# A trunk of two layers on one core: another home for projected blocks, and a PSUM bank for turned tiles

## The chip, the core and the metric

The kernel runs on one core of one Trainium2 chip. The metric is the device time of one execution in microseconds; less is better. TensorE (PE) does matrix products and transposes, VectorE (DVE), ScalarE (ACT) and GpSimd (POOL) the rest, and each engine takes its own instructions in order. DMA queues move data; the queue named SP is issued by SyncE, another here by GpSimd.

## What is computed

256 tokens of width 2048 pass through two layers, each a mixer, cross-attention into 256 memory tokens and a gated feed-forward network, all with a residual and an RMSNorm ahead. The first layer's mixer is split: eight heads of a gated linear recurrence (HGRN2) and eight of a gated delta rule (GDN). The second's is Mamba-2 (SSD, 8 groups). Weights are fp32. Cut to the mixers:

```python
def hgrn2_gdn_mixer(u, w_in, ...):
    a_q, a_f, a_i, a_g, b_q, b_k, b_v, b_g, b_beta, b_a = _split(matmul(u, w_in), HY_SIZES)
    log_f = log(lb + (1.0 - lb) * sigmoid(a_f));  k_a = (1.0 - lb) * sigmoid(-a_f)
    o_a = gated_head_norm(hgrn2_chunked(silu(a_q), k_a, a_i, log_f), hgrn_norm, a_g)
    qkv = silu(causal_depthwise_conv(concatenate([b_q, b_k, b_v]), gdn_conv_w))
    ...
    o_b = gated_head_norm(gated_delta_chunked(l2norm(q_b), l2norm(k_b), v_b, beta, g), gdn_norm, b_g)
    return matmul(concatenate([o_a, o_b]), w_out)
def gated_delta_chunked(...):
    t_mat = triangular_solve(eye + a_mat, eye)
...
def mamba2_mixer(u, w_in, ...):
    z, xbc, dt_raw = _split(matmul(u, w_in), ...)
    xbc = silu(causal_depthwise_conv(xbc, conv_w) + conv_b)
    ...
    return matmul(rmsnorm(y * silu(z), norm_w), w_out)
```

## The kernel before

**Weights.** `wtiles` (L158) streams every weight as raw tiles `wr` of 128x1024 fp32, four buffers, on the SP queue. `split` (L155) makes two of each: ScalarE casts to the short format `wh`, VectorE takes the rest, `wl`. Activations `u` are split likewise. `xstat` multiplies a block of 512 columns in 96 matmuls (16 k tiles, two token halves, three products xh·wh, xl·wh, xh·wl) into two PSUM tiles `acc`. These accumulation matmuls (helper `mm`, L121) are nearly all of TensorE's work. Helpers hide callers: L121 is every matmul, L124 every two-operand product (`tt`), L127 every product of three (`stt`).

**Pools.** PSUM has four banks for `acc` (pool pa) and four in rotation for everything else (pool pm, function `psb`, name `mx` in the rows). In SBUF the small work buffers `b2` (shown as `b`) rotate over four; `tmp` and `sm` over two; `raw`, `vt`, `kq`, `cv`, `gate`, `X`, `XT`, `D` have one each.

**Projected blocks.** `rows` (L355) lets ScalarE scale the two accumulators into two `b2` tiles. `turned` (L272) transposes one such block in two halves on TensorE, eight transposes in all, each half into one of pm's banks. `columns` (L369) makes both halves and returns them. A convolution (`conv`, L347: one ScalarE copy and three VectorE products per 128 channels), or sigmoids, or copies then read them.

**A delta-rule chain.** Each call of `gdn(g)` handles four heads. Products of kq give M (tile MD) and its decays; a scratch write (L554) and a reload (L556) on GpSimd's queue bring the 16x16 diagonal blocks together as U; thirty small VectorE products (15 steps) invert them; a copy (L567), a write (L571) and loads (L573) give X and XT. Then three levels of matmuls join blocks: XT·B, a copy R by ScalarE (L585), X·R and R·X, and a subtraction on VectorE. The products with v, and in `finish` with the decays (`w,MD`, `w,D`), follow, then `head_norm` (L421, L429) and the transposes of its result (`cst,b`). The first chain is `gdn(0)`, the second `gdn(1)`; then the recurrence `hgrn(0)` and `hgrn(1)`, whose six levels take differences of cv into `tmp` on VectorE, an exponential on ScalarE (L660) and two products with kq on GpSimd.

**What sets the order.** The program is written in order of the formulas. A planner with a timeline of its own then decides, engine by engine, in which order instructions stand, and lets the buffers of a pool rotate by it. It mixes accumulation matmuls of later blocks into a chain where it judges a wait.

Of the kernel before, what the change touches and what calls it, by code (L numbers as in the profile page):

```python
# [9 lines left out]
F32 = mybir.dt.float32  # L10
# [3 lines left out]
AF = mybir.ActivationFunctionType  # L14
ALU = mybir.AluOpType
AX = mybir.AxisListType
PSUM = bass.MemoryType.PSUM

P = 128
D = 2048  # L20
T = 256
# [57 lines left out]
def trunk(ctx: ExitStack, tc: tile.TileContext, A: dict, out: bass.AP):  # L79
    nc = tc.nc  # L80
    pe, act, dve, pool = nc.tensor, nc.scalar, nc.vector, nc.gpsimd
# [4 lines left out]
    mp = ctx.enter_context(tc.tile_pool(name="m", bufs=1))  # L86
    dp = ctx.enter_context(tc.tile_pool(name="d", bufs=1, space=bass.MemoryType.DRAM))
    pa = ctx.enter_context(tc.tile_pool(name="pa", bufs=4, space=PSUM))
    pm = ctx.enter_context(tc.tile_pool(name="pm", bufs=4, space=PSUM))


    cols = cp.tile([P, NCOLS], F32, name="cols")
# [23 lines left out]
    def col(name, i=0, n=1):  # L116
        o = COLS[name][0] + i
        return cols[:, o:o + n]
# [10 lines left out]
    def t4(tag, shape, dt=F32):  # L129
        return mp.tile(shape, dt, name=tag, tag=tag, bufs=BUFS.get(tag, 1))  # L130

    def psb(shape=None):
        return pm.tile(shape or [P, 512], F32, name="mx", tag="mx")
# [135 lines left out]

    h = [cp.tile([P, 2, 512], F32, name=f"h{nb}") for nb in range(4)]  # L270

    def turned(src, i):  # L272

        ps = psb([P, 2, T])
        for x in range(2):
            c = 2 * i + x
            for a in range(2):
                pe.transpose(ps[:, x, a * P:(a + 1) * P], src[a][:, c * P:(c + 1) * P], ident)  # L278
        return ps
# [69 lines left out]
    def conv(c, x, w):  # L349

        act.activation(c, x, AF.Copy, scale=w[:, 3:4])  # L351
        for s in range(1, 4):
            stt(c[:, s:T], x[:, 0:T - s], w[:, 3 - s:4 - s], c[:, s:T], ALU.mult, ALU.add)

    def rows(N, W, n0, func=AF.Copy, first=None):  # L355

        accs = xstat(W, n0, 512, N.u)
        if first:
            first()
        r = N.column()  # L360
        o = [t4("b2", [P, 512]) for _ in range(2)]
        for a in range(2):
            act.activation(o[a], accs[a], func, scale=r[:, a:a + 1])  # L363
            if func == AF.Sigmoid:
                stt(o[a], accs[a], r[:, a:a + 1], o[a], ALU.mult, ALU.mult)
        return o

    def columns(N, W, n0, func=AF.Copy):

        o = rows(N, W, n0, func)  # L370
        return [turned(o, i) for i in range(2)]

    def heads_by_token(N, W, n0, c0):

# [77 lines left out]
    def hybrid(N, nxt):  # L452
        W = ("hy_w_in", 0)
# [17 lines left out]
            return decay_parts(gT, 8), bt  # L471

        def conv_in(j, g, o):
            o_rows = rows(N, W, 4096 + 1024 * j + 512 * g, first=constants_in if (j, g) == (1, 0) else None)
            ps = [turned(o_rows, i) for i in range(2)]
            for m in range(4):
                conv(o[:, m, :], ps[m // 2][:, m % 2], col("gdn_conv", 4 * (8 * j + 4 * g + m), 4))

# [141 lines left out]
        def hgrn(g):  # L622
            kq = t4("kq", [P, 2, 4, T])
            lf = t4("tmp", [P, 4, T])
            fs = t4("raw", [P, 4, T])
            for i, ps in enumerate(columns(N, W, 1024 + 512 * g)):
                act.activation(lf[:, 2 * i:2 * i + 2], ps, AF.Sigmoid)
                act.activation(fs[:, 2 * i:2 * i + 2], ps, AF.Sigmoid, scale=-1.0)
            for m in range(4):
                dve.tensor_scalar(kq[:, 0, m], fs[:, m], lb[:, 1, 4 * g + m:4 * g + m + 1], None, op0=ALU.mult)  # L630
            for i, ps in enumerate(columns(N, W, 512 * g, AF.Sigmoid)):
                act.copy(kq[:, 1, 2 * i:2 * i + 2], ps)
            gate = gate_rows(N, W, 3072 + 512 * g, AF.Sigmoid)
            G = t4("cv", [P, 4, T])
# [80 lines left out]

    def xattn(layer, N, nxt):
        q = t4("cv", [P, 4, T])
        for i, ps in enumerate(columns(N, ("xa_wq", layer), 0)):
            act.copy(q[:, 2 * i:2 * i + 2], ps)
        def load_mem(nb):  # L720
            raw = wp.tile([P, 4, T], F32, name="wr", tag="wr", bufs=4)
# [2 lines left out]

        M = Norm(("norm_mem", 16 * layer), load_mem, mem_r[0] if mem_r else None)
        k = t4("X", [P, 4, T])
        for i, ps in enumerate(columns(M, ("xa_wk", layer), 0)):
            act.copy(k[:, 2 * i:2 * i + 2], ps)
        if not mem_r:
            mem_r.append(cp.tile([P, 2], F32, name="mem_r"))  # L730
# [69 lines left out]
    def ssd(N, nxt):  # L800
# [18 lines left out]

        def bc(half):  # L820

            t = [t4(tag, [P, 4, T]) for tag in ("vt", "raw")]
            for j in range(2):
                ps = columns(N, W, 8192 + 1024 * j + 512 * half)
                for x in range(4):
                    b = 32 + 8 * j + 4 * half + x
                    conv(t[j][:, x], ps[x // 2][:, x % 2], col("ssd_conv", 4 * b, 4))
                    act.activation(t[j][:, x], t[j][:, x], AF.Silu, bias=col("ssd_conv_b", b))
            return t

        def group(g, bct):
# [7 lines left out]
            act.copy(cb[:, 1], p0[:, 1])  # L839
            tt(dve, cb[:, 2], p1, le, ALU.mult)  # L840
            xc = t4("cv", [P, 4, T])
            px = columns(N, W, 4096 + 512 * g)
            for m in range(4):
                conv(xc[:, m], px[m // 2][:, m % 2], col("ssd_conv", 4 * (4 * g + m), 4))
                act.activation(xc[:, m], xc[:, m], AF.Silu, bias=col("ssd_conv_b", 4 * g + m))
            xd = t4("w", [P, 2, 8, 64])
            for a in range(2):
                ps = psb([P, 8, 64])
# [5 lines left out]
            for half in range(2):  # L854
# [8 lines left out]
                for x in range(2):  # L863
                    m = 2 * half + x
                    stt(y[:, m], xc[:, m], col("ssd_d", 4 * g + m), ps[:, x], ALU.mult, ALU.add)
            for i, z in enumerate(columns(N, W, 512 * g, AF.Silu)):
                tt(dve, y[:, 2 * i:2 * i + 2], y[:, 2 * i:2 * i + 2], z, ALU.mult)
            hi, lo = utiles()
            for m in range(4):
# [144 lines left out]
```

## Time and profile before

| | us |
|---|---|
| median of three runs | 2999.55 (2998.99 to 3001.03) |
| the profiled execution | 2998.11 |
| its span in the trace | 2996.3 |
| TensorE busy | 2944.5 |
| first delta-rule chain, 160.92 to 201.26 | 40.34 |
| second, 297.51 to 344.46 | 46.95 |
| SSD stage, 730 to 2215 | 1485.00 |

The trace holds one execution. A row gives its start and duration, the operation with the tiles it writes and reads (out<-in), a count, and in square brackets the idle time of the engine ahead of it and what ended that. A stretch that is as long as its PE busy time has no TensorE idle. The granted clock stands as a share of full speed.

### The profile page before, as it was taken

Reading aid. Unit: us, or ns where it says so; the run is one execution under the profiler, and the core shown is the slowest. Engines: PE = TensorE matmul, PEld = TensorE weight load, DVE = VectorE, ACT = ScalarE, POOL = GpSimd, SP = SyncE. Lnnn points to the kernel's source line nnn. Section 1 sums busy time; section 2 is a strip of 40 time slices with the busy share of each in tenths; the row PEclk is TensorE's granted clock in tenths of the full one; section 3 lists DMA queues with packets and bytes.
Section 4 is the critical chain, followed back from the end, with each engine's and each line's share of the span. In section 5 each row is a group of like instructions: output and inputs, shape, how many; then the busy total and the mean of one; then the engine's idle time right before and its main releaser. Section 6 shows DMA issues by size and latency. Waiting matters only on the chain.

```text
span 2996.3 us, 36590 instructions
## 1 busy us (share of the span) xinstructions
PE 2944.5 (98%) x13948; PEld 2450.2 (82%) x13948; DVE 1735.7 (58%) x2154; ACT 1486.4 (50%) x1916; POOL 262.7 (9%) x209
## 2 busy tenths in 40 slices
PE   9989899999999999999999999999999999999998
PEld 7877788887888888888888888888888888888887
DVE  6647566666455455545667655667665554545455
ACT  7435455465443444344556645666555444443444
POOL 1011223020000000000012300232000000000000
PEclk9999899999999999999999999999999999999999
DMA  7535245564655666665555555545666666666664
GB/s 277 177 116 178 69 136 163 177 209 140 191 190 190 193 188 188 195 190 188 175 176 157 156 186 187 163 153 164 185 201 188 190 189 191 192 188 192 193 189 148
DMA packets 152160, 533.35 MB, mean 178 GB/s; under 512 B 16592, under 2 KB 22864, under 8 KB 151984
## 3 DMA queue, kind: packets, MB, share of 16 engines
q1 hardware_dynamic: 150096, 526.15, 56.3%
q0 software_dynamic: 1472, 4.59, 0.5%
q8 instruction: 109, 1.79, 0.2%
q14 instruction: 67, 0.55, 0.1%
q10 hardware_dynamic: 416, 0.27, 0.0%
HBM read 526.49 MB, written 4.46 MB: 177 GB/s over the span
## 4 chain that ended last, share of the span: by engine, by line
PE 94%; DMA 2%; DVE 1%; ACT 1%; issue 1%; POOL 0%; DVEq 0%; SPq 0%; ACTq 0%; POOLq 0%
PE acc L121 86%; PE mx L121 6%; PE mx L278 2%; DMA XT<-scratch 0%; DVE wl L124 0%; DMA scratch<-b 0%; POOL tmp L124 0%; DMA wr<-in_memT 0%; DMA b<-scratch 0%; ACT b L585 0%; PE mx L850 0%; DMA scratch<-MD 0%; DVE b L124 0%; PE mx L429 0%; DMA wr<-in_hy_w_in 0%
## 5 line engine op out<-in xcount | busy, mean ns | idle before, releaser
L121 PE MATMUL acc<-wh,u 128*128 128x512 f32 (+1 forms) x7904 | 2450.4, 390 | 7.0 <-ACT wh L156 7.0
L124 DVE TENSOR_TENSOR wl<-wr,wh 128x1024 fp32r<-128x1024 f32 x980 | 1243.2, 1272 | 1055.1 <-ACT wh L156 1052.8
L121 PEld LDWEIGHTS acc<-wh,u 128*128 128x128 f32 x7904 | 1480.1, 188 | 305.2 <-ACT wh L156 7.8
L156 ACT CAST wh<-wr 128x1024 fp32r<-128x1024 f32 x980 | 1029.1, 1052 | 1165.1 <-PE acc L121 1104.3
L121 PE MATMUL acc<-wl,u 128*128 128x512 f32 (+1 forms) x3952 | 1536.5, 389 | 1.3 <-DVE wl L124 1.3
L121 PEld LDWEIGHTS acc<-wl,u 128*128 128x128 f32 x3952 | 744.4, 188 | 150.8 <-DVE wl L124 2.9
L124 POOL TENSOR_TENSOR tmp<-gh,cst 128x512 fp32r<-128x512 f32 x36 | 39.9, 1110 | 1317.9 <-ACT gh L156 884.7
L124 POOL TENSOR_TENSOR tmp<-tmp,kq 128x512 f32<-128x512 f32 x32 | 56.9, 1805 | 136.5 <-ACT tmp L660 124.4
L127 DVE SCALAR_TENSOR_TENSOR cv<-mx,cols,cv 128x255 f32<-128x255 f32 (+2 forms) x120 | 52.5, 475 | 13.6 <-ACT cv L351 13.0
L124 DVE TENSOR_TENSOR h<-h,acc 128x512 f32<-128x512 f32 (+1 forms) x84 | 52.2, 655 | 9.6 <-PE acc L121 9.4
L363 ACT ACTIVATE b<-acc,r 128x512 f32<-128x512 f32 x66 | 43.9, 687 | 27.0 <-PE acc L121 16.9
L124 POOL TENSOR_TENSOR tmp<-gl,cst 128x512 fp32r<-128x512 f32 x36 | 52.4, 1457 | 0.1
L127 DVE SCALAR_TENSOR_TENSOR u<-mx,cols,u 128x256 fp32r<-128x256 f32 x96 | 42.7, 478 | 14.4 <-ACT u L436 7.3
L299 ACT ACTIVATE u<-mx,cols 128x256 fp32r<-128x256 f32 x80 | 34.2, 469 | 20.9 <-PE mx L278 17.9
L278 PE MATMUL mx<-cst,b 128*128 128x128 f32 x272 | 39.1, 274 | 0.0
L124 DVE TENSOR_TENSOR u<-mx,u 128x512 fp32r<-128x512 f32 x48 | 31.0, 683 | 13.9 <-ACT u L156 13.9
L124 DVE TENSOR_TENSOR X<-X,mx 128x512 f32<-128x512 f32 x28 | 18.5, 683 | 32.9 <-PE mx L121 32.9
L278 PEld LDWEIGHTS mx<-cst,b 128*128 128x128 f32 x272 | 32.3, 141 | 5.9 <-issue 1.4
L156 ACT CAST u<-mx 128x512 fp32r<-128x512 f32 x48 | 26.0, 591 | 22.3 <-PE mx L121 11.7
L124 POOL TENSOR_TENSOR MD<-MD,b 128x1536 f32<-128x1536 f32 x8 | 35.0, 4371 | 7.8 <-ACT MD L403 7.8
L121 PE MATMUL mx<-tmp,mr 128*128 128x512 f32 x108 | 32.7, 406 | 0.0
L121 PEld LDWEIGHTS mx<-tmp 128*128 128x128 f32 x240 | 28.8, 196 | 2.5 <-POOL tmp L124 1.9
(259 smaller groups left out, 1281.1 us busy)
## 6 DMA issues: line engine op xcount, KB each, us to landing
wr<-in_ffn_w_gate SPq DMA_DIRECT2D x176, 512.0 KB, 3.7
wr<-in_ffn_w_up SPq DMA_DIRECT2D x176, 512.0 KB, 3.6
wr<-in_ffn_w_down SPq DMA_DIRECT2D x176, 512.0 KB, 3.7
wr<-in_ssd_w_in SPq DMA_DIRECT2D x162, 512.0 KB, 3.8
wr<-in_hy_w_in SPq DMA_DIRECT2D x130, 512.0 KB, 4.2
wr<-in_ssd_w_out SPq DMA_DIRECT2D x64, 512.0 KB, 3.9
wr<-in_hy_w_out SPq DMA_DIRECT2D x32, 512.0 KB, 3.7
wr<-in_xa_wq SPq DMA_DIRECT2D x16, 512.0 KB, 3.7
```

Source lines behind the costliest of these rows:

```text
L121: pe.matmul(o, lhsT=lhsT, rhs=rhs, start=start, stop=stop, skip_group_check=True)
L124: e.tensor_tensor(o, a, b, op=op)
L127: dve.scalar_tensor_tensor(o, a, s, b, op0=op0, op1=op1)
L156: act.copy(hi, src)
L278: pe.transpose(ps[:, x, a * P:(a + 1) * P], src[a][:, c * P:(c + 1) * P], ident)
L299: act.activation(hi[:, c], ps[:, x], AF.Copy, scale=g)
L363: act.activation(o[a], accs[a], func, scale=r[:, a:a + 1])
```

## The change

The change gives the projected blocks and the turned tiles other buffers:

- `rows` writes its block into one tile `raw` ([128, 2, 512], a single buffer) in place of two `b2` tiles.
- PSUM's pool pm goes from four banks to three, and a new pool pt has one, for the turned tiles (name `tn`).
- `columns` becomes a generator: it turns the first half, hands it to its reader, then turns the second into the same bank. All its readers loop over it.
- In `hgrn` the tile that was `raw` goes: the sigmoid is written into kq and scaled there. In SSD's `bc` the second tile moves from `raw` to `gate`.

```diff
--- before.py
+++ after.py
@@ -86,7 +86,8 @@
     mp = ctx.enter_context(tc.tile_pool(name="m", bufs=1))
     dp = ctx.enter_context(tc.tile_pool(name="d", bufs=1, space=bass.MemoryType.DRAM))
     pa = ctx.enter_context(tc.tile_pool(name="pa", bufs=4, space=PSUM))
-    pm = ctx.enter_context(tc.tile_pool(name="pm", bufs=4, space=PSUM))
+    pt = ctx.enter_context(tc.tile_pool(name="pt", bufs=1, space=PSUM))
+    pm = ctx.enter_context(tc.tile_pool(name="pm", bufs=3, space=PSUM))
 
 
     cols = cp.tile([P, NCOLS], F32, name="cols")
@@ -269,9 +270,10 @@
 
     h = [cp.tile([P, 2, 512], F32, name=f"h{nb}") for nb in range(4)]
 
-    def turned(src, i):
-
-        ps = psb([P, 2, T])
+    def turned(src, i, ps=None):
+
+        if ps is None:
+            ps = psb([P, 2, T])
         for x in range(2):
             c = 2 * i + x
             for a in range(2):
@@ -358,17 +360,19 @@
         if first:
             first()
         r = N.column()
-        o = [t4("b2", [P, 512]) for _ in range(2)]
+        o = t4("raw", [P, 2, 512])
+        o = [o[:, 0], o[:, 1]]
         for a in range(2):
             act.activation(o[a], accs[a], func, scale=r[:, a:a + 1])
             if func == AF.Sigmoid:
                 stt(o[a], accs[a], r[:, a:a + 1], o[a], ALU.mult, ALU.mult)
         return o
 
-    def columns(N, W, n0, func=AF.Copy):
-
-        o = rows(N, W, n0, func)
-        return [turned(o, i) for i in range(2)]
+    def columns(N, W, n0, func=AF.Copy, first=None):
+
+        o = rows(N, W, n0, func, first)
+        for i in range(2):
+            yield i, turned(o, i, pt.tile([P, 2, T], F32, name="tn", tag="tn"))
 
     def heads_by_token(N, W, n0, c0):
 
@@ -471,10 +475,10 @@
             return decay_parts(gT, 8), bt
 
         def conv_in(j, g, o):
-            o_rows = rows(N, W, 4096 + 1024 * j + 512 * g, first=constants_in if (j, g) == (1, 0) else None)
-            ps = [turned(o_rows, i) for i in range(2)]
-            for m in range(4):
-                conv(o[:, m, :], ps[m // 2][:, m % 2], col("gdn_conv", 4 * (8 * j + 4 * g + m), 4))
+            for i, ps in columns(N, W, 4096 + 1024 * j + 512 * g, first=constants_in if (j, g) == (1, 0) else None):
+                for x in range(2):
+                    m = 2 * i + x
+                    conv(o[:, m, :], ps[:, x], col("gdn_conv", 4 * (8 * j + 4 * g + m), 4))
 
 
 
@@ -622,13 +626,12 @@
         def hgrn(g):
             kq = t4("kq", [P, 2, 4, T])
             lf = t4("tmp", [P, 4, T])
-            fs = t4("raw", [P, 4, T])
-            for i, ps in enumerate(columns(N, W, 1024 + 512 * g)):
+            for i, ps in columns(N, W, 1024 + 512 * g):
                 act.activation(lf[:, 2 * i:2 * i + 2], ps, AF.Sigmoid)
-                act.activation(fs[:, 2 * i:2 * i + 2], ps, AF.Sigmoid, scale=-1.0)
-            for m in range(4):
-                dve.tensor_scalar(kq[:, 0, m], fs[:, m], lb[:, 1, 4 * g + m:4 * g + m + 1], None, op0=ALU.mult)
-            for i, ps in enumerate(columns(N, W, 512 * g, AF.Sigmoid)):
+                act.activation(kq[:, 0, 2 * i:2 * i + 2], ps, AF.Sigmoid, scale=-1.0)
+            for m in range(4):
+                dve.tensor_scalar(kq[:, 0, m], kq[:, 0, m], lb[:, 1, 4 * g + m:4 * g + m + 1], None, op0=ALU.mult)
+            for i, ps in columns(N, W, 512 * g, AF.Sigmoid):
                 act.copy(kq[:, 1, 2 * i:2 * i + 2], ps)
             gate = gate_rows(N, W, 3072 + 512 * g, AF.Sigmoid)
             G = t4("cv", [P, 4, T])
@@ -715,7 +718,7 @@
 
     def xattn(layer, N, nxt):
         q = t4("cv", [P, 4, T])
-        for i, ps in enumerate(columns(N, ("xa_wq", layer), 0)):
+        for i, ps in columns(N, ("xa_wq", layer), 0):
             act.copy(q[:, 2 * i:2 * i + 2], ps)
         def load_mem(nb):
             raw = wp.tile([P, 4, T], F32, name="wr", tag="wr", bufs=4)
@@ -724,7 +727,7 @@
 
         M = Norm(("norm_mem", 16 * layer), load_mem, mem_r[0] if mem_r else None)
         k = t4("X", [P, 4, T])
-        for i, ps in enumerate(columns(M, ("xa_wk", layer), 0)):
+        for i, ps in columns(M, ("xa_wk", layer), 0):
             act.copy(k[:, 2 * i:2 * i + 2], ps)
         if not mem_r:
             mem_r.append(cp.tile([P, 2], F32, name="mem_r"))
@@ -819,13 +822,13 @@
 
         def bc(half):
 
-            t = [t4(tag, [P, 4, T]) for tag in ("vt", "raw")]
+            t = [t4(tag, [P, 4, T]) for tag in ("vt", "gate")]
             for j in range(2):
-                ps = columns(N, W, 8192 + 1024 * j + 512 * half)
-                for x in range(4):
-                    b = 32 + 8 * j + 4 * half + x
-                    conv(t[j][:, x], ps[x // 2][:, x % 2], col("ssd_conv", 4 * b, 4))
-                    act.activation(t[j][:, x], t[j][:, x], AF.Silu, bias=col("ssd_conv_b", b))
+                for i, ps in columns(N, W, 8192 + 1024 * j + 512 * half):
+                    for x in (2 * i, 2 * i + 1):
+                        b = 32 + 8 * j + 4 * half + x
+                        conv(t[j][:, x], ps[:, x % 2], col("ssd_conv", 4 * b, 4))
+                        act.activation(t[j][:, x], t[j][:, x], AF.Silu, bias=col("ssd_conv_b", b))
             return t
 
         def group(g, bct):
@@ -839,10 +842,10 @@
             act.copy(cb[:, 1], p0[:, 1])
             tt(dve, cb[:, 2], p1, le, ALU.mult)
             xc = t4("cv", [P, 4, T])
-            px = columns(N, W, 4096 + 512 * g)
-            for m in range(4):
-                conv(xc[:, m], px[m // 2][:, m % 2], col("ssd_conv", 4 * (4 * g + m), 4))
-                act.activation(xc[:, m], xc[:, m], AF.Silu, bias=col("ssd_conv_b", 4 * g + m))
+            for i, px in columns(N, W, 4096 + 512 * g):
+                for m in (2 * i, 2 * i + 1):
+                    conv(xc[:, m], px[:, m % 2], col("ssd_conv", 4 * (4 * g + m), 4))
+                    act.activation(xc[:, m], xc[:, m], AF.Silu, bias=col("ssd_conv_b", 4 * g + m))
             xd = t4("w", [P, 2, 8, 64])
             for a in range(2):
                 ps = psb([P, 8, 64])
@@ -863,7 +866,7 @@
                 for x in range(2):
                     m = 2 * half + x
                     stt(y[:, m], xc[:, m], col("ssd_d", 4 * g + m), ps[:, x], ALU.mult, ALU.add)
-            for i, z in enumerate(columns(N, W, 512 * g, AF.Silu)):
+            for i, z in columns(N, W, 512 * g, AF.Silu):
                 tt(dve, y[:, 2 * i:2 * i + 2], y[:, 2 * i:2 * i + 2], z, ALU.mult)
             hi, lo = utiles()
             for m in range(4):
```

The numbers of matmuls, VectorE and GpSimd instructions and SP transfers stay. ScalarE has 78 table loads in place of 61, 16 of the 17 more in SSD, two a group. The lines shift by one to four. The planner gives a different order; three places matter.

The first is TensorE at the start of the first chain (`acc` rows are other blocks' accumulation matmuls, `XT,b` the chain's first step of a level). Before:

```order
L121 MATMUL acc<-wh,u 128x512 x2
L121 MATMUL acc<-wl,u 128x512
L121 MATMUL acc<-wh,u 128x512
L121 MATMUL mx<-XT,b_1128 128x128 x4
L121 MATMUL mx<-X,b_1135 128x128 x4
L121 MATMUL mx<-b_1135,X 128x128 x4
L121 MATMUL mx<-XT,b_1149 128x128 x4
L121 MATMUL mx<-X,b_1156 128x128 x4
L121 MATMUL mx<-b_1156,X 128x128 x4
L121 MATMUL mx<-XT,b_1170 128x128 x4
```

After:

```order
L122 MATMUL acc<-wl,u 128x512
L122 MATMUL mx<-XT,b_1128 128x128 x4
L122 MATMUL acc<-wh,u 128x512 x2
...
L122 MATMUL acc<-wl,u 128x512
L280 MATMUL tn<-cst,raw 128x128 x4
L122 MATMUL acc<-wh,u 128x512 x2
...
L122 MATMUL acc<-wl,u 128x512
L122 MATMUL mx<-X,b_1135 128x128 x4
L122 MATMUL mx<-b_1135,X 128x128 x4
L122 MATMUL mx<-XT,b_1149 128x128 x4
```

Before, 22 rows of the chain stand without anything between; now groups of 9 to 49 accumulation matmuls stand between its steps, and 49 before `head_norm`'s transposes. From the last product on kq to the first `XT,b` stand 157 accumulation matmuls before, and 165 and 12 transposes after.

The second is VectorE at the products on U (`b` is U and its inverse, `kq<-tn` the convolution). Of the first chain, before:

```order
L124 TENSOR_TENSOR b_1086<-b_1085,b_1083 64x3x13
L124 TENSOR_TENSOR b_1085<-b_1085,b_1086 64x3x13
L124 TENSOR_TENSOR wl<-wr,wh 128x1024
L124 TENSOR_TENSOR b_1086<-b_1085,b_1083 64x4x12
L124 TENSOR_TENSOR b_1085<-b_1085,b_1086 64x4x12
L124 TENSOR_TENSOR b_1086<-b_1085,b_1083 64x5x11
L124 TENSOR_TENSOR b_1085<-b_1085,b_1086 64x5x11
L124 TENSOR_TENSOR b_1086<-b_1085,b_1083 64x6x10
L124 TENSOR_TENSOR b_1085<-b_1085,b_1086 64x6x10
```

After:

```order
L125 TENSOR_TENSOR b_1086<-b_1085,b_1083 64x3x13
L125 TENSOR_TENSOR b_1085<-b_1085,b_1086 64x3x13
L125 TENSOR_TENSOR b_1086<-b_1085,b_1083 64x4x12
L125 TENSOR_TENSOR b_1085<-b_1085,b_1086 64x4x12
L128 SCALAR_TENSOR_TENSOR kq<-tn,cols,kq 128x255
L125 TENSOR_TENSOR b_1086<-b_1085,b_1083 64x5x11
L128 SCALAR_TENSOR_TENSOR kq<-tn,cols,kq 128x254
L125 TENSOR_TENSOR b_1085<-b_1085,b_1086 64x5x11
L125 TENSOR_TENSOR wl<-wr,wh 128x1024
L128 SCALAR_TENSOR_TENSOR kq<-tn,cols,kq 128x253
L125 TENSOR_TENSOR b_1086<-b_1085,b_1083 64x6x10
```

Nine convolution products and one more `wl` came in among the thirty. In the second chain eight `wl` stand there in place of five, with two scalings of kq, two products `raw<-acc`, four scans and four differences `tmp<-cv` besides. There, 145 accumulation matmuls stand from the last product on kq to the first `XT,b` before, and 155 and 12 transposes after. On GpSimd two products `tmp<-gh` and `tmp<-gl` now stand between the loads of X and of XT in the first chain, and four `tmp<-tmp,kq` of the recurrence's first two levels ahead of the write of `b` in the second.

The third is TensorE at the end of the second chain (`w,D` are `finish`'s products, `cst,b` the transposes behind `head_norm`). Before:

```order
L121 MATMUL mx<-vt,X 128x128 x4
L121 MATMUL mx<-w,MD 128x128 x4
L121 MATMUL mx<-vt,X 128x128 x4
L121 MATMUL mx<-w,D 128x128 x12
L429 MATMUL mx<-cst,b_2334 128x128 x3
L121 MATMUL acc<-wh,u 128x512
```

After:

```order
L122 MATMUL mx<-vt,X 128x128 x4
L122 MATMUL mx<-w,MD 128x128 x4
L122 MATMUL mx<-vt,X 128x128 x4
L122 MATMUL mx<-w,D 128x128 x12
L122 MATMUL acc<-wh,u 128x512
L122 MATMUL acc<-wl,u 128x512
L122 MATMUL acc<-wh,u 128x512 x2
L122 MATMUL acc<-wl,u 128x512
L122 MATMUL acc<-wh,u 128x512 x2
```

Forty accumulation matmuls now stand between `w,D` and the transposes; the rest of the chain is as unbroken as before. Behind it, ScalarE's copy of the recurrence's value block (`vt<-acc`) stands after seven exponentials.

## Rows read from the trace of the kernel before

**Rows 1.** The page: each engine's busy time, share of the span, instructions.
```profile
PE 2944.5 (98%) x13948; PEld 2450.2 (82%) x13948; DVE 1735.7 (58%) x2154; ACT 1486.4 (50%) x1916; POOL 262.7 (9%) x209
```

**Rows 2.** Windows: length, busy of PE PEld DVE ACT POOL, clock, DMA, GB/s.
```profile
160.92:201.26 40.34, 29.49 (x210) 26.49 (x211) 13.79 (x33) 9.15 (x16) 7.06 (x6) 0.96 0.12 41
...
297.51:344.46 46.95, 33.09 (x211) 29.80 (x211) 14.43 (x34) 9.16 (x14) 5.06 (x4) 0.85 0.12 41
...
730.00:2215.00 1485.00, 1485.00 (x6977) 1229.76 (x6976) 864.29 (x960) 764.15 (x986) 138.94 (x103) 1.00 0.58 181
```

**Rows 3.** The chain that ended last, in order of time: start, duration, what.
```profile
124.89 0.79 DVE MD L127 x2
...
136.69 1.21 DVE wl L124
...
154.65 7.06 DMA XT<-scratch
...
902.07 147.39 PE acc L121 x650
```

**Rows 4.** Timeline of TensorE in the first chain.
```profile
161.84 1.13 PE L121 MATMUL mx<-XT,b 128*128 128x128 f32 x8 [0.92 <-DMA XT<-scratch]
163.65 1.16 PE L121 MATMUL mx<-X,b 128*128 128x128 f32 x8 [0.68 <-ACT b L585]
164.64 1.06 PE L121 MATMUL mx<-b,X 128*128 128x128 f32 x8
...
186.78 2.84 PE L121 MATMUL mx<-w,D 128*128 128x128 f32 x24
193.79 1.05 PE L429 MATMUL mx<-cst,b 128*128 128x128 f32 x3 [4.17 <-DVE b L127]
```

**Rows 5.** Windows with the columns of rows 2: two spells of half clock.
```profile
193.70:197.11 3.41, 3.32 (x9) 2.63 (x10) 1.84 (x8) 0.00 (x0) 0.00 (x0) 0.50 0.00 0
299.50:309.74 10.24, 7.54 (x32) 6.98 (x32) 1.63 (x3) 0.59 (x2) 1.26 (x1) 0.50 0.37 122
```

**Rows 6.** Timeline of TensorE: start of the second chain, and the recurrence.
```profile
301.44 2.05 PE L121 MATMUL mx<-XT,b 128*128 128x128 f32 x8 [3.93 <-DMA XT<-scratch]
...
370.13 2.11 PE L121 MATMUL mx<-tmp 128*128 128x64 f32 x13 [1.76 <-POOL tmp L124]
```

**Rows 7.** Timeline of GpSimd: first chain's scratch write, then the second's two.
```profile
125.67 1.54 POOL L554 DMA_DIRECT2D scratch<-MD  x2 [41.53 <-DVE MD L127]
...
264.98 1.56 POOL L554 DMA_DIRECT2D scratch<-MD  x2 [24.74 <-DVE MD L127]
...
287.78 1.67 POOL L571 DMA_DIRECT2D scratch<-b  x2 [15.08 <-issue]
```

**Rows 8.** VectorE, 60 to 560: shapes, count, busy us, mean ns, idle before.
```profile
L124 DVE TENSOR_TENSOR tmp<-cv 128x512 f32<-128x512 f32 x28 | 21.2, 800 | 0.0
...
L640 DVE TENSOR_TENSOR_SCAN cv<-big,tmp 128x128 f32<-128x128 f32 x16 | 5.5, 404 | 2.5 <-ACT tmp L637 2.5
...
L127 DVE SCALAR_TENSOR_TENSOR kq<-mx,cols,kq 128x255 f32<-128x255 f32 x12 | 5.3, 477 | 3.3 <-ACT kq L351 3.3
...
L127 DVE SCALAR_TENSOR_TENSOR b<-acc,r,b 128x512 f32<-128x512 f32 x4 | 2.9, 740 | 6.9 <-ACT b L363 6.9
```

**Rows 9.** GpSimd by line, 60 to 560, columns as in rows 8.
```profile
L124 POOL TENSOR_TENSOR tmp<-tmp,kq 128x512 f32<-128x512 f32 x32 | 56.9, 1805 | 136.5 <-ACT tmp L660 124.4 <-ACT kq L632 7.3 <-ACT tmp L663 4.7
...
L124 POOL TENSOR_TENSOR tmp<-gh,cst 128x512 fp32r<-128x512 f32 x4 | 6.0, 1510 | 103.0 <-ACT gh L156 57.0 <-PE mx L121 46.0
```

**Rows 10.** Timeline of VectorE beside GpSimd's products in the recurrence.
```profile
374.03 3.24 DVE L124 TENSOR_TENSOR tmp<-cv 128x512 f32<-128x512 f32 x2
```

**Rows 11.** Timeline of TensorE in SSD: transposes between accumulation matmuls.
```profile
1403.64 0.82 PE L278 MATMUL mx<-cst,h 128*128 128x128 f32 x6
```

**Rows 12.** ScalarE by line in 1540 to 1732 of SSD, columns as in rows 8.
```profile
L156 ACT CAST wh<-wr 128x1024 fp32r<-128x1024 f32 x57 | 59.5, 1050 | 31.9 <-PE acc L121 31.9
L396 ACT ACT_TABLE_LOAD x8 | 10.3, 1283 | 0.1
```

## The prediction

> **What bounds the kernel now.** I read the page first: TensorE is busy 98% of the span, VectorE 58%, ScalarE 50% [rows 1]. So an edit is worth only what it gives TensorE: idle time filled, or time at the lower clock regained. The stage table comes next: the reader compares the length of a stretch with its PE busy time. In the 1485 us of the SSD stage the two are equal: nothing can be gained there, only lost [rows 2]. The idle time that the change can reach lies above all in two delta-rule chains: 40.34 − 29.49 = 10.85 us and 46.95 − 33.09 = 13.86 us [rows 2].
>
> Idle time is not the whole loss: matmuls that depend on one another also run with gaps. So I count what a chain holds. An accumulation matmul takes 147.39/650 = 0.2268 us [rows 3]; one of 128x128 takes (2.84 − 1.06)/(24 − 8) = 0.111 us, from a row of 24 and a row of 8 [rows 4]. Each chain stretch holds 176 chain records, 16 transposes and 18 accumulation matmuls: 192 × 0.111 + 18 × 0.2268 = 25.4 us. The first stretch thus **loses 14.9 us**, the second **21.5**. Of the first, 0.92 is the wait for XT's load, 4.17 the wait for head_norm before the last transposes, the rest short hops to ScalarE and VectorE [rows 4] and a spell of 3.41 us at a granted clock of 0.50, the lower of its two levels (1.2 GHz), right behind that wait, which costs half its length, 1.7 [rows 5]. The second has 3.93 for XT [rows 6], again 4.17 in head_norm, and two spells at 0.50, of 10.24 us [rows 5] and of 3.41.
>
> What decides the wait for XT is a path beside TensorE, from M's scratch write to XT's arrival. In the first chain: GpSimd issues at 125.67 [rows 7], VectorE then does thirty small products on U with matmul weights' `wl` between them, GpSimd writes and reloads, and XT lands at 154.65 + 7.06 = 161.71 [rows 3]: **36.0 us**. In the second: 264.98 [rows 7] to 301.3 [rows 6]: **36.3 us**. TensorE covers it with accumulation matmuls: 157 in the first chain (35.6 us), 145 in the second (32.9). It has a start of about 0.8 us, the two products that VectorE does last on MD [rows 3]. That gives waits of 36.0 − 34.8 = 1.2 and 36.3 − 32.1 = 4.2, where the rows show 0.92 and 3.93: the sum runs 0.3 too high, and I take that off below.
>
> **The change part by part.** Counts of matmuls, products and transfers stay; the order moves, and ScalarE gets 17 more table loads.
>
> *First chain.* Its first matmul now stands 165 accumulation matmuls and 12 transposes behind the last product on kq: 37.4 + 1.3 − 0.8 = 37.9 us of cover. Between all later steps stand 9 to 49 accumulation matmuls, and 49 before the last transposes: at 0.2268 each, 2.0 to 11.1 us, more than any hop (about 0.7) or the 4.17 [rows 4]. So the hops and the head_norm wait go. The path grows, though. Among the U products VectorE has nine products of the convolution more, 9 × 0.477 = 4.3 [rows 8], and one `wl` more, 1.2 [rows 3]. On GpSimd two products, of 1.51 the first [rows 9] and the second as large a tile, 3.0 together, stand between the issues of X and XT: queued behind them is XT's load, and TensorE waits for that. XT's transfer then no longer queues behind X's, so the cost may be less: 0.5 to 3.0; I take 2.3, nearer to the upper end, since GpSimd works in order. Path 36.0 + 4.3 + 1.2 + 2.3 = 43.8; wait 43.8 − 37.9 − 0.3 = 5.6. A half-clock spell behind such a wait costs 1.7 as now. Left of the 14.9: 7.3. **Gain 7.6.** Bounds: 14 if the nine products fit into VectorE's pauses, 3 if the wait brings the long spell.
>
> *Second chain.* It stays unbroken. Its cover is 155 accumulation matmuls and 12 transposes, 35.2 + 1.3 − 0.8 = 35.7. VectorE gets into the U products three `wl` (3.6), two scalings (a scan's length at most, 0.8), two sigmoid products at 0.74, four scans at 0.404 and four differences at 0.8 [rows 8], 10.7 in all; the mean of the differences holds slow ones beside GpSimd [rows 10], so I take 10.0. Path 46.3, wait 46.3 − 35.7 − 0.3 = 10.3, **6.4 more than now**. Against this 40 accumulation matmuls (9.1 us) now cover the head_norm wait (−4.2) and its spell (−1.7). ScalarE's copy of the recurrence's value block stands behind seven exponentials, so two PSUM accumulators stay taken longer: 0 to 1.8 by the nearest wait [rows 6], I take 1.0. **Cost 1.5**, range −8 (gain, no new work on the path) to +9 (GpSimd on it too, below).
>
> *The recurrence.* GpSimd's products of the first two levels now stand ahead of the second chain; the 1.76 wait at 370.13 [rows 6] and the half-clock spell that follows it, another 1.7, go: **gain 3.5**. Next late there is VectorE's `wl` for the matmuls, with no wait of a microsecond now.
>
> *Everywhere else.* A transposes group is cut in two by the single turned bank: six in a row took 0.82 [rows 11], eight 1.06 [rows 4], 0.12 for each more, so starting anew costs next to nothing while matmuls stand between; 0.6 in all for some thirty blocks. With pm at three banks nothing else waits there in the order. The table loads, 17 × 1.283 = 21.8 us of ScalarE, sit mostly in SSD; per group ScalarE now waits 31.9/3.6 = 8.9 us for TensorE's accumulators (57 casts in the stretch, 16 to a group: 3.6 groups) against 2 × 1.283 = 2.6 [rows 12]. I cost them at nothing, under a cover of 8.9 a group.
>
> By the rows a switch costs 1.283. The Trainium skill's "ScalarE: Activation LUTs", section "What ACT_TABLE_LOAD costs", adds a drain of about 1.38 us to each: by it a group would pay 5.3, still below 8.9, so the sum is the same by either, with less slack. This trace speaks against the drain: ahead of its eight loads ScalarE idled 0.1 us in all [rows 12].
>
> **Sum:** −7.6 + 1.5 − 3.5 + 0.6 = −9.0. The profiled execution took 2998.11 (span 2996.3): 2989.1. The median of the runs shown, 2999.55, lies 1.44 above it, so **2990.5 us**; own range 2984 to 2995.
>
> **The rivals.**
> *Nothing gained* (3001). The paths are longer than I think, since VectorE and GpSimd get in each other's way. For it: the differences at 374.03, beside GpSimd's product, took 1.62 each [rows 10] where the mean is 0.80 [rows 8]. In the second chain four GpSimd products of 1.8 [rows 9] stand ahead of the write of `b`: up to 7.2 us, if their exponentials come late. And behind a first-chain wait of 5.6 the half clock may last 10.24 as in the second chain [rows 5], costing 3.4 more. Then −4.2 + (1.5 + 7.2) − 3.5 + 0.6 = +1.6, 3001.1. Against it: GpSimd stood still for 15 us before that write [rows 7].
> The Trainium skill's "SBUF — State Buffer", section "Who interferes with whom", has a VectorE instruction with two SBUF inputs contend with a GpSimd one that reads SBUF; the row at 374.03 agrees. By that rule all four products would fall on U's path, and the time would be this rival's.
>
> *Slower* (3011). In SSD the one `raw` and one turned bank serialise each block: copy, two transposes, reads, next. If ScalarE reaches the copy late, TensorE's next block finds its accumulators taken. Price: the two loads per group, 8 × 2.6 = 20.5, straight on TensorE: −9.0 + 20.5 = +11.5. It decides once ScalarE's 8.9 of slack per group is used up; against it that slack, and 0.00 idle now [rows 2].
>
> *More gained* (about 2976). The first chain doesn't wait at all (−14.9), and the second's wait for XT stays 3.9 with no new wait, so only its head_norm wait and spell go (−5.9): −14.9 − 5.9 − 3.5 + 0.6 = −23.7, 2975.8. It needs U's products to lose nothing to what is put between them. For it: VectorE is busy 58% of the span [rows 1], so it has pauses that the added products could fall into. Against it: these stand inside the row of U's products, which follow one another at once.
>
> **How the numbers follow.** Forecast 0.48, nothing gained 0.25, slower 0.14, more gained 0.13. The range leaves out the slower case and half of "more gained", 0.2: 2976 to 3004. About 0.2%, 6 us, is what a measurement of this kernel can tell from no change: bounds 2993.6 and 3005.6. Faster: 0.13 and most of the forecast, 0.54. Same: the 0.25 and the forecast's upper end, 0.33. Slower: 0.13.
>
> **What would show it.** Right: the first `mx<-XT,b` of the first chain after a wait of 4 to 7, no hop waits of 0.7 behind it, no 4.17 before its last transposes; the second chain's XT wait near 10 with hops of 0.7 kept and no 4.17; no wait at the first level of the recurrence; SSD without TensorE idle. Wrong: an XT wait under 2 in the first chain, one above 15 in the second, half-clock spells where none is now, or idle time in SSD behind ScalarE.

## The result: 4 us slower where a gain of 9 was forecast

| | us |
|---|---|
| before, median of 20 runs | 2998.94 (2993.5 to 3001.34) |
| after, median of 20 runs | 3003.01 (3000.55 to 3007.72) |
| ratio | 1.0017, 95% interval 1.001 to 1.0024 |
| span in the trace, before and after | 2996.3 and 2999.6 |

The changed kernel is 4.1 us slower: less than the 6 us that the prediction counted as no change, though the interval lies wholly above 1. The forecast was 2990.5, and faster. The time lies inside the wide range, 2976 to 3004, and outside the forecast's own, 2984 to 2995.

The page of the changed kernel reads almost as [rows 1]:

```profile
PE 2951.6 (98%) x13948; PEld 2448.5 (82%) x13948; DVE 1739.2 (58%) x2154; ACT 1513.3 (50%) x1933; POOL 265.2 (9%) x209
```

TensorE idles less than before, 48.0 us in place of 51.8, and is busy 7.1 longer with the same matmuls. So a reader who looks for idle time alone finds no loss here. Windows of the changed kernel, with the columns of [rows 2]: the first chain, the second, most of SSD, the second cross-attention.

```profile
160.00:205.00 45.00, 45.00 (x261) 39.23 (x260) 30.82 (x43) 23.30 (x31) 13.45 (x13) 1.00 0.58 176
320.00:366.00 46.00, 30.36 (x187) 26.97 (x188) 17.47 (x32) 7.92 (x11) 11.08 (x11) 0.85 0.33 106
1537.30:2145.70 608.40, 608.40 (x2901) 492.50 (x2900) 384.02 (x454) 379.58 (x527) 125.58 (x97) 1.00 0.54 166
2192.00:2260.00 68.00, 62.72 (x285) 51.20 (x284) 39.24 (x59) 34.14 (x65) 0.00 (x0) 0.92 0.51 154
```

The first chain has no idle time left. The second idles 15.64 us, the second cross-attention 5.28.

To see what a stage loses beyond its matmuls, I took each trace's start times and subtracted what its matmuls take back to back: 0.2268 us for one of accumulation (0.1195 with 256 columns), 0.110, 0.216 and 0.43 for other records that stream 128, 256 and 512 columns, and 1.50/16 for the 64-column products shown below. Stages are cut at equal counts of accumulation matmuls (500, 950 and 1668 for the chains, 2164 to 2400, 2400 to 8480, 8480 to 8750), so they hold the same weights in every kernel. The table has what is left, in us, for the kernels of this study (the labels are explained below). What counts is the difference between two kernels; in the chains some us of it can be chance, as raw_loop and b_loop below show. The traced execution lies within about 2 us of its kernel's median, but that of raw_pm3 5.2 above.

| stage | before | after | raw_only | pt_only | xd_swap | xa_loop_k | raw_pm3 | raw_loop | b_loop |
|---|---|---|---|---|---|---|---|---|---|
| first chain and what follows | 15.6 | 0.7 | 14.5 | 28.1 | 1.3 | 0.7 | 27.2 | 12.1 | 17.9 |
| second chain, recurrence | 28.1 | 32.8 | 25.6 | 44.9 | 34.6 | 35.9 | 24.0 | 23.1 | 26.4 |
| first cross-attention | 8.7 | 8.4 | 3.5 | 8.6 | 8.7 | 1.5 | 7.8 | 0.7 | 1.5 |
| first FFN, SSD | 5.4 | 12.5 | 5.6 | 15.2 | 6.9 | 6.9 | 7.5 | 5.6 | 5.4 |
| second cross-attention | 1.6 | 9.7 | 1.6 | 10.2 | 9.2 | 1.4 | 8.1 | 0.7 | 0.6 |
| whole trace, the rest with it | 82.1 | 85.3 | 73.3 | 129.7 | 83.7 | 69.2 | 97.4 | 68.3 | 74.6 |

Everything up to the end of the first cross-attention became 12.0 us shorter. SSD then gave back 7.1 and the second cross-attention 8.1. Neither stood in the sum.

**Where SSD loses, without idle time.** TensorE in one of SSD's eight groups, the kernel after:

```profile
1548.38 0.65 PE L122 MATMUL mx<-D,w 128*64 128x256 f32 x2
1548.96 0.50 PE L122 MATMUL mx<-tmp,mr 128*128 128x512 f32 x1
1549.39 1.52 PE L122 MATMUL mx<-D,w 128*64 128x128 f32 x14
1550.84 0.97 PE L122 MATMUL mx<-tmp,mr 128*128 128x512 f32 x3
```

And the same sixteen records of the kernel before:

```profile
1555.37 1.57 PE L121 MATMUL mx<-D,w 128*64 128x256 f32 x16
1556.87 1.44 PE L121 MATMUL mx<-tmp,mr 128*128 128x512 f32 x5
```

From the first record to what follows the group it took 1.50 us before. Now a matmul on `tmp,mr`, 128 columns wide, stands behind the first product's two records, and the group takes 2.46, of which that matmul accounts for 0.24. The cut costs 0.72, in each of the eight groups: 5.8 us. These products use 64 columns of the array each, and the product of an even head goes to the other 64 than that of an odd one. In an unbroken group pairs of records start 0.01 to 0.06 us apart and share their time; in the cut one most stand 0.10 to 0.22 apart, and the first two, which have no partner, take 0.58. The Trainium skill's "TensorEngine Tiling (Array Packing)", section "Key Properties", says that different tiles of the array can work in parallel and that changing the tiling mode drains TensorE. The trace agrees with the first: 1.50 for the pairs. The 0.72 that a full-width matmul between them costs fits the second, but it holds the lost pairs too (0.31 at the first two records), and no run here tells the two apart.

**Where the second cross-attention loses.** TensorE of the kernel after:

```profile
2217.67 0.38 PE L758 MATMUL mx<-cst,kq 128*128 128x128 f32 x2
2217.89 0.60 PE L122 MATMUL mx<-X,cv 128*128 128x256 f32 x2
2218.32 0.82 PE L758 MATMUL mx<-cst,kq 128*128 128x128 f32 x6
2218.97 1.75 PE L122 MATMUL mx<-X,cv 128*128 128x256 f32 x6
2225.32 1.94 PE L758 MATMUL mx<-cst,kq 128*128 128x128 f32 x8 [4.59 <-DVE kq L754]
2227.92 2.05 PE L122 MATMUL mx<-D,XT 128*128 128x256 f32 x4 [0.66 <-DVE D L759]
```

`X,cv` are scores, `cst,kq` transposes of probabilities. No accumulation matmul is left behind the last scores, so their whole softmax shows: a wait of 4.59, and a spell at half clock that begins inside it (window, columns as above):

```profile
2222.60:2232.84 10.24, 6.86 (x20) 5.55 (x21) 2.68 (x8) 2.21 (x9) 0.00 (x0) 0.50 0.12 48
```

Before, 22 accumulation matmuls stood there, with 1.10 of idle time in all and no such spell:

```profile
2218.39 1.89 PE L121 MATMUL mx<-X,cv 128*128 128x256 f32 x8
...
2225.12 1.03 PE L755 MATMUL mx<-cst,kq 128*128 128x128 f32 x8
2227.26 1.10 PE L121 MATMUL mx<-D,XT 128*128 128x256 f32 x4 [1.10 <-DVE D L756]
```

### The profile page after: what moved, and what is told of

It is laid out like the page before. It is cut to its first block, busy times and chain, and to the rows that moved or that the text cites. A ratio compares the mean times of both kernels' runs of the same rounds, so it can differ in the third digit from the quotient of the medians.

```text
span 2999.6 us, 36568 instructions
## 1 busy us (share of the span) xinstructions
PE 2951.6 (98%) x13948; PEld 2448.5 (82%) x13948; DVE 1739.2 (58%) x2154; ACT 1513.3 (50%) x1933; POOL 265.2 (9%) x209
## 3 DMA queue, kind: packets, MB, share of 16 engines
q0 software_dynamic: 1472, 4.59, 0.5%
## 4 chain that ended last, share of the span: by engine, by line
PE 93%; issue 2%; DVE 1%; DMA 1%; POOL 1%; ACT 1%; SPq 0%; DVEq 0%; ACTq 0%; POOLq 0%
PE acc L122 86%; PE mx L122 5%; PE mx L280 1%; PE tn L280 1%; POOL tmp L125 1%; DVE wl L125 0%; DMA wr<-in_memT 0%; DVE b L125 0%; PE mx L853 0%; DMA XT<-scratch 0%; DMA b<-scratch 0%; DMA scratch<-b 0%; DMA wr<-in_hy_w_in 0%; PE mx L758 0%; DVE tmp L125 0%
## 5 line engine op out<-in xcount | busy, mean ns | idle before, releaser
L125 POOL TENSOR_TENSOR tmp<-gh,cst 128x512 fp32r<-128x512 f32 x36 | 49.6, 1379 | 1303.2 <-ACT gh L157 849.3
L128 DVE SCALAR_TENSOR_TENSOR cv<-tn,cols,cv 128x255 f32<-128x255 f32 (+2 forms) x120 | 57.7, 481 | 31.3 <-ACT cv L353 28.6
L366 ACT ACTIVATE raw<-acc,r 128x512 f32<-128x512 f32 x66 | 43.5, 684 | 10.7 <-PE acc L122 10.6
L280 PE MATMUL tn<-cst,raw 128*128 128x128 f32 x272 | 45.5, 275 | 0.0
L280 PEld LDWEIGHTS tn<-cst,raw 128*128 128x128 f32 x272 | 35.0, 142 | 9.5
L125 POOL TENSOR_TENSOR tmp<-gl,cst 128x512 fp32r<-128x512 f32 x36 | 40.3, 1120 | 0.1
L122 PE MATMUL mx<-tmp 128*128 128x64 f32 (+1 forms) x240 | 29.5, 281 | 2.0 <-POOL tmp L125 2.0
```

What stands on the lines that cost most here:

```text
L122: pe.matmul(o, lhsT=lhsT, rhs=rhs, start=start, stop=stop, skip_group_check=True)
L125: e.tensor_tensor(o, a, b, op=op)
L128: dve.scalar_tensor_tensor(o, a, s, b, op0=op0, op1=op1)
```

## The experiments

The theory behind them: the home `raw` and the bank split do different things. The home frees the planner to put other work into the chains; the split with its single turned bank moves SSD's and cross-attention's steps. The rivals: SSD loses through ScalarE's 16 added table loads or the single `raw`; or cross-attention waits for something else than the softmax. Each kernel was timed beside the kernel before, on two chips: the runs up to xa_loop_k on one, the last three on the other.

**raw_only and pt_only: one part each.** raw_only keeps pm's four banks and turns both halves at once:

```diff
-        o = [t4("b2", [P, 512]) for _ in range(2)]
+        o = t4("raw", [P, 2, 512])
+        o = [o[:, 0], o[:, 1]]
```

with the moves in `hgrn` and `bc` that the tile `raw` needs. pt_only is the changed kernel with `rows` writing into `b2` as before, and `hgrn` and `bc` using `raw` as before.

> Only the home `raw` (with the moves in hgrn and bc that it needs); turned tiles stay in pm's four banks, both halves at once. Theory (the losses in SSD and in the second cross-attention come from the bank split, the gain from the home): SSD and second cross-attention as in the kernel before, within 1 us; the order puts 7 to 22 accumulation matmuls between the levels of both chains but leaves head_norm's wait of 4.2 in both, so each chain loses about 7 less; first cross-attention 3 less: 2985, 2980 to 2990. Rival (the single buffer `raw` and ScalarE's switches make SSD slower): the 7 us of SSD stay, 2992 or more.

> Only the bank split: pt one bank, pm three, halves turned one by one; blocks stay in `b2`. Theory: SSD +7 and the second cross-attention +7.4 as in the changed kernel, with the D,w groups cut by a 512-wide matmul in all eight groups. The chains' covers shrink from 157 to 109 and from 145 to 21 accumulation matmuls, so XT's waits grow by 48 x 0.2268 = 10.9 and 124 x 0.2268 = 28; head_norm's waits go, 18 matmuls cover them: -11.8. Sum +42: 3040, 3030 to 3050. Rival (the split is harmless in SSD and cross-attention): 15 less, 3025, with SSD free of loss.

raw_only: 2989.85 us beside 2998.99, ratio 0.9972 (0.996 to 0.9983). pt_only: 3045.96, ratio 1.0157 (1.0143 to 1.0171). On SSD and the second cross-attention the theory holds against its rival in both: raw_only keeps them as before (5.6 and 1.6), pt_only has the losses of the changed kernel (15.2 and 10.2; in SSD 2.7 more, with two waits of 1.10 for `w` inside the groups on D). So the split alone makes these losses. The home alone makes 9 us of gain, but not where I had put it: the first chain loses 1.1 less and the second, with the recurrence, 2.5 less, where I had 7 for each; 5.2 lie in the first cross-attention, where 11 accumulation matmuls now stand behind the last scores instead of none. In the first chain head_norm's wait has a half-clock spell of 6.83 us behind it, where I had counted 3.41, and a wait of 1.25 for the copy into `raw` is new. TensorE in raw_only's first chain:

```profile
161.26 1.13 PE L121 MATMUL mx<-XT,b 128*128 128x128 f32 x8 [1.68 <-DMA XT<-scratch]
...
169.03 1.06 PE L121 MATMUL mx<-XT,b 128*128 128x128 f32 x8
174.92 1.05 PE L121 MATMUL mx<-X,b 128*128 128x128 f32 x8
...
209.92 1.11 PE L430 MATMUL mx<-cst,b 128*128 128x128 f32 x4 [4.18 <-DVE b L127]
```

Accumulation matmuls fill the hops (5 us from 169.03 to 174.92), but head_norm's wait stays. Of these kernels it goes only in those with both parts: the first chain's gain (0.7 in place of 15.6) is the work of the two together. In pt_only the chains' covers shrink to 109 and 21 accumulation matmuls, and the second waits for XT:

```profile
331.45 2.05 PE L122 MATMUL mx<-XT,b 128*128 128x128 f32 x8 [21.49 <-DMA XT<-scratch]
```

I had priced that at 32 and its head_norm waits as gone; the wait is 21.49, the head_norm waits of 4.18 stayed, and the sum came out 6 too low. The parts don't add: −9 and +47 would make +38, and the changed kernel measures +4. What the split costs in the chains it costs only without the home.

**xd_swap: the cut in SSD undone.** The changed kernel with SSD's second token half of `xd` made first:

```diff
             xd = t4("w", [P, 2, 8, 64])
-            for a in range(2):
+            for a in (1, 0):
```

The planner had cut the group because the first product on D needs only the first half of `xd`, and the second half came late: with one turned bank the convolution's second half is turned only when the first is read.

> The changed kernel with one edit: SSD makes the second token half of xd first, so that both halves are there when the first product on D can start. The order then has no 512-wide matmul inside the D,w groups, and the same 78 table loads. Theory (the cut of the D,w groups is what SSD lost): 8 x 0.73 = 5.8 less, 2997; SSD stands 1.2 above the kernel before. Rival (table loads or the single buffers): SSD keeps its 7 us, 3003.

2998.59 us beside 2998.99, ratio 0.9999 (0.999 to 1.0008). I had expected 2997, the rival 3003. SSD's loss falls from 12.5 to 6.9, with the same 78 table loads. All D,w groups are whole again:

```profile
1553.56 1.57 PE L122 MATMUL mx<-D,w 128*64 128x256 f32 x16
1555.06 1.20 PE L122 MATMUL mx<-tmp,mr 128*128 128x512 f32 x4
```

5.6 of SSD's 7.1 were the cut; the table loads can't have cost TensorE more than the 1.5 that is left.

**xa_loop_k: the softmax covered.** xd_swap, and in cross-attention

```diff
                     act.activation(pr[:, a, m], ps[:, x], AF.Exp, bias=mx[:, m:m + 1], scale=sc,
                                    accum_out=sm[:, m:m + 1])
             dve.reciprocal(sm, sm)
             for m in range(4):
                 dve.tensor_scalar(pr[:, a, m], pr[:, a, m], sm[:, m:m + 1], None, op0=ALU.mult)
+        for a in range(2):
             for b in range(2):
```

with k's halves turned in pm's banks.

> xd_swap with two more edits in cross-attention: all scores before the transposes of the probabilities, and k's block turned in pm's banks. In the second cross-attention 33 accumulation matmuls and 8 transposes, 8.4 us, stand between the last scores and the last transposes, in the first 22, 5.0 us. Theory (the softmax after the last scores, some 6 to 8 us, is uncovered there): second cross-attention 7 less, first 5 less than in the changed kernel: 2985, 2981 to 2990. Rival (the wait is for something else, such as the values' block): 2997 as xd_swap.

2983.23 us beside 2998.99, ratio 0.9949 (0.9937 to 0.9962). The first cross-attention loses 7 less, the second 8 less. TensorE in the second:

```profile
2203.15 1.02 PE L122 MATMUL mx<-X,cv 128*128 128x256 f32 x4
...
2212.48 1.03 PE L759 MATMUL mx<-cst,kq 128*128 128x128 f32 x8
2214.17 1.10 PE L122 MATMUL mx<-D,XT 128*128 128x256 f32 x4 [0.66 <-DVE D L760]
```

Nothing waits at 2212.48. It was the softmax, and the half clock that went with the wait. For the second cross-attention no run tells the loop from the move of k's halves; for the first, b_loop below has the loop alone, and the same gain.

**raw_pm3, raw_loop, b_loop: which part of the split, and what the change is worth.** raw_pm3 is raw_only with `bufs=3` for pm and no turned bank; raw_loop is raw_only, b_loop the kernel before, each with the loop of xa_loop_k.

> raw_only with three banks in pm in place of four and no bank for turned tiles (one bank stays empty); halves are turned both at once. It tells the single turned bank from the missing fourth bank. Theory (the turned bank, which lets the second half start only when the first is read, makes xd's second half late and cuts the D,w groups): SSD as in raw_only, 4.2 us above its matmuls. Rival (three banks are too few): SSD 11. In the second cross-attention 5 accumulation matmuls, 1.1 us, are left behind the last scores, so either way 5 to 7 more than raw_only there; the second chain stands unbroken again, 5 to 8 more: 3003, 2997 to 3010.

> raw_only with the scores of both token halves ahead of the transposes in cross-attention. In the first cross-attention 41 accumulation matmuls, 9.3 us, stand behind the last scores instead of 11: 2 less there, nothing in the second: 2988, 2985 to 2990. Rival (the first cross-attention's loss is not the softmax): 2990.

> The kernel before with the scores of both token halves ahead of the transposes in cross-attention, nothing else. 33 accumulation matmuls, 7.5 us, stand behind the last scores of the first cross-attention instead of none: 7 less there, nothing in the second: 2992, 2989 to 2995. Taken with xa_loop_k it tells what the change is worth without its two side effects: xa_loop_k should be 8 to 9 less.

raw_pm3: 3008.23 us beside 2998.35, ratio 1.0038 (1.0025 to 1.005). Three banks without the turned one leave the groups on D whole. Of its products, by shape (columns as in [rows 8]), from 1400 to 2150, first the kernel after:

```profile
L122 PE MATMUL mx<-D,w 128*64 128x256 f32 x64 | 15.5, 392 | 0.0
...
L122 PE MATMUL mx<-D,w 128*64 128x128 f32 x64 | 11.3, 279 | 0.0
```

then raw_pm3:

```profile
L121 PE MATMUL mx<-D,w 128*64 128x256 f32 x64 | 10.5, 397 | 0.0
...
L121 PE MATMUL mx<-D,w 128*64 128x128 f32 x64 | 6.7, 272 | 0.0
```

So the cut comes from the single turned bank. Three banks cost 2 us in SSD in another way, 1.25 of it one wait for `wl`. In the second cross-attention, though, three banks are enough to uncover the softmax (8.1, with a wait of 3.54 for it). The two parts of the split thus share the blame. The time is 5 above my expectation. In the trace raw_pm3's first chain loses 13 more than raw_only's, with a wait of 3.34 for XT, one of 3.28 before the next blocks' transposes and longer half-clock spells, and its second chain none of the 5 to 8 that I had expected; since this execution took 5.2 more than the median, part of the 13 can be chance.

raw_loop: 2984.32 us, ratio 0.9953 (0.9941 to 0.9966). b_loop: 2990.65, ratio 0.9972 (0.9962 to 0.9982). The loop gives about 7 in the first cross-attention of the kernel before, as expected. xa_loop_k is then 7.4 below b_loop, 6.9 by the two ratios (I had expected 8 to 9), so the change, with its two side effects mended, is worth about that. But raw_loop, without any bank split, has the same time as xa_loop_k within their intervals. Both beat both kernels of this case.

raw_loop came out 4 below its expectation. Its instructions stand in the same order as raw_only's up to the cross-attention, yet its chains lose 5 less: the first wait for XT was 0.50 in place of 1.68, and the half-clock spells behind the waits were shorter. b_loop, in the order of the kernel before, loses 2.3 more in the first chain; the changed kernel, xd_swap and xa_loop_k, again in one order there, lose 32.8, 34.6 and 35.9 in the second chain and the recurrence. So a single trace fixes the loss of a chain only to some microseconds.

## Why the prediction was wrong, step by step

**First chain: right way, gain too small.** I forecast a path of 43.8 us and a wait of 5.6; the trace shows no wait. GpSimd's queue after, the path's steps:

```profile
135.92 0.75 POOL L558 DMA_DIRECT2D scratch<-MD  x1 [3.88 <-DVE MD L128]
139.86 0.84 POOL L560 DMA_DIRECT2D b<-scratch  x1 [3.19 <-DMA scratch<-MD]
...
159.25 1.69 POOL L575 DMA_DIRECT2D scratch<-b  x2 [16.45 <-DVE kq L128]
163.71 1.54 POOL L577 DMA_DIRECT2D X<-scratch  x2 [2.77 <-DMA scratch<-b]
165.27 1.99 POOL L125 TENSOR_TENSOR tmp<-gh,cst 128x512 fp32r<-128x512 f32 x1
167.23 1.03 POOL L125 TENSOR_TENSOR tmp<-gl,cst 128x512 fp32r<-128x512 f32 x1
168.21 1.54 POOL L577 DMA_DIRECT2D XT<-scratch  x2
```

The last write of M stands at 135.92, and the records of the queue's transfers have XT's first half landing at 172.04: 36.1 us. Counted in the same way, from the last write of M (126.46), it was 35.3 before; my 36.0 began at the first. So the path grew by 0.8, not by 7.8: it is the term that was mis-sized. U's products grew by 3.3 (from the landing of U at 143.2 to 159.25, against 135.4 to 148.1), not by 5.5. The two GpSimd products did stand there, 3.0 as I took them, but XT's transfer took 3.8 instead of 7.06, and the write and reload of U 1.7 less. The cover, from the last product on kq at 134.85 to XT's matmul at 173.98, is 39.1, as forecast (38.7 before I took off the start). So all 14.9 us went, not 7.6. What made the transfers faster was not tried. For XT the landings fit what the prediction said of X's transfer: before, X's second half landed at 159.75, 5.1 behind XT's issue, and XT 2.0 after it; now it lands at 169.51, 1.3 behind XT's issue. I had given this at most the 2.5 between 3.0 and 0.5; XT's transfer gained 3.2.

**Second chain: the wait nearly right, in part by luck.** The forecast wait was 10.3:

```profile
338.11 2.04 PE L122 MATMUL mx<-XT,b 128*128 128x128 f32 x8 [9.19 <-DMA XT<-scratch]
```

with hops of 0.7 kept and no wait for head_norm. A spell of 13.65 us at half clock stands at it; before, one of 10.24 and one of 3.41 ([rows 5] has the long one). Counted as in the table, but for this chain alone, it loses 20.7 us where it lost 21.9, and I had +1.5; the spread above is larger than that. The wait came out through errors that cancel. VectorE beside GpSimd's products of the recurrence:

```profile
308.96 9.69 POOL L125 TENSOR_TENSOR tmp<-tmp,kq 128x512 f32<-128x512 f32 x4 [10.89 <-ACT tmp L663]
...
311.43 3.19 DVE L125 TENSOR_TENSOR b<-b,b 64x55 f32<-64x55 f32 x3
...
315.68 3.80 DVE L125 TENSOR_TENSOR b<-b,b 64x63 f32<-64x63 f32 x5
...
320.55 1.66 DVE L125 TENSOR_TENSOR b<-b,b 64x63 f32<-64x63 f32 x7
```

Four of U's products took 1.45 to 1.55 us there, in place of 0.21, and each ended 0.07 behind one of GpSimd's four: 5.1 more, which my path left out. The products put between U's cost 9.0 in place of 10.0, U's other products took 0.8 less, and the cover holds a wait of 1.31 for `wl` that I hadn't counted. The 1.0 that I gave two accumulators shows in no wait.

**The recurrence: wrong sign.** I let the wait for GpSimd and its half-clock spell go (−3.5). TensorE after:

```profile
402.00 2.57 PE L122 MATMUL mx<-tmp 128*128 128x64 f32 x16 [0.99 <-POOL tmp L125]
...
446.30 0.50 PE L122 MATMUL acc<-wl,u 128*128 128x512 f32 x1 [2.10 <-DVE wl L125]
480.65 2.70 PE L122 MATMUL mx<-tmp 128*128 128x64 f32 x16 [0.98 <-POOL tmp L125]
```

The wait moved to the next levels: four of GpSimd's products (394.00, 7.95 us) end just before 402.00. `wl` came late at 446.30, where I had said no wait of a microsecond stood. A spell of half clock follows each, 3.41 long: 4.1 of waiting and up to 3 x 1.7 = 5.1, against 1.76 and 1.7 before. By the start times the recurrence loses about 4 more than before. The step that failed is "Next late there is VectorE's `wl` for the matmuls, with no wait of a microsecond now": I moved the first two levels and left the others as if nothing stood ahead of them.

These errors nearly cancel, which is luck: up to the end of the first cross-attention the trace gains 12.0 (1.1 of it before the first chain, which no term of mine touched), where the terms summed to −9.6.

**Everywhere else: the step that turned the result.** The step that failed is "With pm at three banks nothing else waits there in the order", and 0.6 for the rest, against 7.1 in SSD and 8.1 in the second cross-attention, 15.2 measured. I compared counts of instructions in SSD and cross-attention and the waits of before, but not who stands next to whom. Both losses stood in the order: a full-width matmul inside the groups on D, and no accumulation matmul behind the second cross-attention's last scores. The rival "slower" had the right place, SSD, and the wrong mechanism: its table loads cost at most 1.5 of its 20.5. There was no TensorE idle in SSD, as I had asked for, and yet it lost; so that mark proved nothing. Of the signs of being wrong, two came: an XT wait under 2 in the first chain (there was none), and half-clock spells where none was, such as the one in the second cross-attention.

**The rivals.** "More gained" was right on the first chain (−14.9). "Nothing gained" came nearest in time, 3001, by a wrong way. Its contention of VectorE with GpSimd in the second chain was there, 5.1 of the 7.2 that it priced, but other terms made up for it (9.19 against my 10.3 without it). GpSimd's four products were done at 318.65, before the last of U's, so they didn't delay the write of `b` themselves. The long half clock behind a wait in the first chain didn't come, since there was no wait.

## What to carry to other kernels

When a change moves a planner's order, compare the neighbours of each dependent step in every stage, also in stages that the edit doesn't aim at and where the engine never idles. A group of narrow matmuls that run side by side is one unit: a full-width one inside it costs time that no wait shows. And take the parts of a change apart: here one part alone gave 9 us, and with the other beside it more than the gain was lost in two other stages.

## What the runs showed that I had not expected

- TensorE at 100% busy can lose time: sixteen records of 64-column products took 1.50 us unbroken and 2.22 with one 128-column matmul among them (its own 0.24 taken off).
- The same order of instructions gives a different loss in a chain from run to run: raw_only and raw_loop differ by 5 us over the two chains, among others through a wait for XT of 1.68 or 0.50 and the half-clock spells behind the waits.
- One scratch load of XT took 7.06 us from issue to landing before, close behind X's, and 3.8 after, of the same size, with X's nearly landed.
- Small VectorE products of 0.21 us took up to 1.55 beside GpSimd's of the recurrence, while `wl` beside the same ones kept its 1.21.
